# RWKV's block inverse on quarters of the array, transfers and norms set apart, and a new order of the jobs

## The chip, the cores and the metric

The kernel runs on one core of one Trainium2 chip. The metric is the device time of one execution in microseconds. TensorE is called PE here, VectorE DVE, ScalarE ACT, GpSimd POOL and SyncE SP; SP issues every DMA of this kernel.

## The reference, cut to what matters

Two layers of a decoder trunk over 512 tokens of width 1024. Five token mixers read columns of one input projection; their outputs are gated, merged, projected, normed and added to x.

```python
for l in range(DEPTH):                                   # DEPTH = 2
    h = rms_norm(x, norm_pre[l])
    cols = jnp.einsum('bsd,dn->bsn', h, w_in[l])         # 1024 x 9668
    ys = (rwkv7_branch(...), dsa_branch(...), retention_branch(...), s5_branch(...), memory_branch(...))
    merged = sum(gates[:, :, i] * jnp.einsum('bsw,wd->bsd', ys[i], w_branch[l, i]) for i in range(5))
    out = jnp.einsum('bsd,de->bse', merged, w_out[l])
    x = x + rms_norm(out, norm_post[l])

# rwkv7_branch, per token t and head:
sa = jnp.einsum('bhvk,bhk->bhv', state, -kk_t)
state = state * w_t + sa[..., None] * (kk_t * a_t) + v_t[..., None] * k_t
```

The RWKV state is carried in chunks of 128 tokens, which needs the inverse of a unit triangular 128 by 128 matrix for each of 4 heads and 4 chunks.

## The kernel before, in words

The program is written by a planner that runs while the kernel is built. `dense()` yields dense jobs (each one is a column block of a weight matrix times the 512 tokens), and `run()` puts steps of "lanes" between them: the branches, the setup, and the norms at a layer's end. The tables `ORDER` and `LANES` give the first order of jobs and lanes, `LAG` is how far ACT and DVE may lag behind PE before lanes pause. What comes out is one fixed order of instructions for each engine. A `yield` in a lane is a place where other work may come between.

A weight piece goes this way: SP loads 256 KB into one of 5 buffers `raw`; ACT casts it to `wh`, DVE subtracts to get the rest `wl` (4 buffers each); PE multiplies `wh` and `wl` with the high and low part of the tokens (`hh`, `hl`), three products that add up in PSUM. SP works in order: a DMA that has to wait for an engine or for a free buffer holds up all that stand behind it. So do DVE, ACT and POOL.

The places that the change touches:

- In `branch_rwkv` the inverse is built from 32 by 32 diagonal blocks (`X`, transposed into `Z`). The next level needs, for each of 4 matrices `u` and each half `b` of the 128 rows, the product of three 32 by 32 blocks. The kernel before multiplies whole 128 by 128 matrices (`N` with `Z`, then `X` with `W`), and masks the product with the constant `lev32`.
- `s5_tables` builds phase tables `sar` on POOL and DVE by doubling, stores them to DRAM (`s5tab`, four DMAs of 256 KB), and loads `sBt`. In the profile the small operands of the doubling are `sem`, `sea`, `seb` and `sta`.
- `finish_out` ends a layer for 128 tokens: `rs` (named `ors`) scales the projected row, `x` is updated, and `put_hT` norms it for the next layer: a square and sum on ACT (`xn`, `xrs`), a power on POOL, a scaled copy on DVE (`xn`), transposes on PE, and the split into `hh` and `hl`. Then `x` is stored to `xs`.
- At the very start, two tiles of x, the row `npre` and the constants are loaded, then five weight pieces.

Of the kernel before, what the change touches and what calls it, by code (L numbers as in the profile page):

```python
# [31 lines left out]
CW2 = float(np.float32(np.round((TWO_PI - CW1) * 2.0 ** 21) / 2.0 ** 21))  # L32
CW3 = float(np.float32(TWO_PI - CW1 - CW2))
MAGIC = 12582912.0
LAG = 11.5
EARLY = -1.0
MAXL = 6
NBUF = {"c1": 10, "c2": 14, "c4": 16, "c16": 2, "raw": 5, "w": 4}
ADD_G = 1.2
ORDER = ("rsg rv w wg g0 xq xsg di su dsg ssg dq g4 g2 dk mem1 dv g3 mem g1",  # L40
         "xsg dq g0 w di rsg wg g4 su dsg ssg dk dv g3 g1 g2")
LANES = ("ret idx>4 s5>4 ms1>3 rwkv dsa ms0 tab x>2", "idx>4 dsa>0 tab ret x rwkv>t s5")


def shape_constants():

    p = np.arange(128)
    c = {}
    c["ident"] = np.eye(128)
    up = (p[:, None] < p[None, :]) * 1.0  # L50
    c["upper"] = np.concatenate([up, up + np.eye(128)], 1)
    c["lev32"] = ((p[:, None] // 64 == p[None, :] // 64) & (p[:, None] % 64 < 32) & (p[None, :] % 64 >= 32)) * 1.0
    c["lower"] = (p[:, None] > p[None, :]) * 1.0
    c["causal"] = np.where(p[None, :] <= p[:, None], 0.0, NEG)
    inv = (10000.0 ** (-np.arange(32, dtype=np.float32) / np.float32(32))).astype(np.float32)
    c["invf"] = inv[p % 32][:, None]
    sgn = np.where(p % 64 < 32, -1.0, 1.0)
    c["sgn"] = sgn[:, None]
    sel = np.zeros((128, 2, 128))
    for j in range(2):  # L60
        for h in range(4):
            sel[h, j] = (p // 64 + 2 * j == h)
    c["sel"] = sel.reshape(128, 256)
    c["bo2"] = (p[:, None] // 64 == np.arange(2)[None, :]) * 1.0
    hd = RET_LOGG[2 * np.arange(2)[None, :] + p[:, None] // 64]
    c["qdec"] = np.exp(hd[:, :, None] * (p + 1)[None, None, :]).reshape(128, 256)
    c["kdec"] = 0.125 * np.exp(hd[:, :, None] * (127 - p)[None, None, :]).reshape(128, 256)
    rel = p[None, :] - p[:, None]
    c["rdecay"] = np.concatenate([np.where(rel >= 0, np.exp(RET_LOGG[2 * j + q] * np.maximum(rel, 0)), 0.0) * 0.125
                                  for q in range(2) for j in range(2)], 1)  # L70
    names = list(c)
    offs, o = {}, 0
    for n in names:
        offs[n] = (o, c[n].shape[1])
        o += c[n].shape[1]
    return np.concatenate([c[n] for n in names], 1).astype(np.float32), offs
# [146 lines left out]
def hybrid_kernel(ctx: ExitStack, tc: tile.TileContext, x, mem, positions, norm_pre, norm_post, norm_mem, w_in,  # L223
# [55 lines left out]
        return t  # L279

    x0 = [load_x(0, 0)]
    ncst = COFF["qdec"][0]
    cst = cp.tile([128, ncst], F32, name="cst")
    nci = COFF["ident"][1]
    assert COFF["ident"][0] == 0 and CONST.shape[1] == ncst + 1024
    SY.dma_start(cst[:, :nci], const[:, :nci])
    x0.append(load_x(0, 1))
    npre = {0: bcast_row(norm_pre[0], "npre")}

    def K(n):  # L290
        o, w = COFF[n]
        return cst[:, o:o + w]
# [810 lines left out]
            yield  # L1103


    def wsb(name, shape, dt=F32, bufs=2):
        return sb(name, shape, dt, bufs, "r")

    def rwkv_epi(l, t0):

# [17 lines left out]
    def branch_rwkv(l):  # L1128
# [87 lines left out]
        rks = sb("wrks", [128, 4, 4])  # L1216
        V.tensor_copy(rks, pss)
        yield
        lev = K("lev32")
        upper = K("upper").rearrange("p (a t) -> p a t", a=2)  # L1220
        M = [wsb("wM", [128, 2, 128]) for _ in range(2)]
        Ms = wsb("wMs", [128, 2, 128])
# [58 lines left out]
        for c in range(4):  # L1281
# [10 lines left out]
                T.transpose(ps[:, u, :], X[:, u, :], ident)  # L1292
            A.copy(Z, ps)
            yield
            ps = psb((128, 4, 128))
            for u in range(4):
                T.matmul(ps[:, u, :], N[u], Z[:, u, :])
            W = wsb("wW", [128, 4, 128])
            V.tensor_tensor(W, ps, lev[:, None, :].to_broadcast([128, 4, 128]), op=OP.mult)
            yield  # L1300
            ps = psb((128, 4, 128))
            for u in range(4):
                T.matmul(ps[:, u, :], X[:, u, :], W[:, u, :])
            V.tensor_tensor(Z, ps, Z, op=OP.add)
            ps = psb((128, 2, 2, 128))
            for a, src in enumerate((B, Kt)):
                for j in range(2):
# [122 lines left out]
    def s5_tables(l):  # L1430
# [35 lines left out]
        for r_ in range(2):  # L1466
            for b in range(2):
                SY.dma_start(s5d["tab"][2 * l + b][:, r_], tab[r_][:, 4 * b:4 * b + 4].rearrange("p b m -> p (b m)"))

        Bt = sb("sBt", [128, 2, nb, 16])  # L1470
        Cs = sb("sCs", [128, 2, nb, 16])
        for r_, w in enumerate((s5_b_re, s5_b_im)):
            bv = w[l].rearrange("(b q) p c -> q p b c", q=2)
            for q in range(2):
                SY.dma_start(Bt[64 * q:64 * q + 64, r_], bv[q])
        yield
        for b in range(2):
# [301 lines left out]
    def finish_out(l, i):  # L1779

        u, rr, xi = (a[i % 2] for a in ST[l, "fin", i // 2])
        rs = sb("ors", [128, 1])
        V.tensor_tensor(rs, rr[:, 0:1], rr[:, 1:2], op=OP.add)
        V.scalar_tensor_tensor(rs, rr[:, 2:3], 16e-6, rs, op0=OP.add, op1=OP.add)
        rsq(rs, rs)
        yield
        for a in range(2):
            o = slice(512 * a, 512 * a + 512)
            V.scalar_tensor_tensor(xi[:, o], u[:, o], rs, xi[:, o], op0=OP.mult, op1=OP.add)
            if l == L - 1:  # L1790
                yield
                SY.dma_start(outr[:, i, o], xi[:, o])
        if l < L - 1:
            yield from put_hT(l + 1, i, xi)
            SY.dma_start(xs[:, i, :], xi)

# [100 lines left out]
    def first_h(i):  # L1897
        if i >= 2:
            x0.append(load_x(0, i))
            yield  # L1900
        yield from put_hT(0, i, x0[i])

    lanes = [Lane(lambda i=i: first_h(i), ("t01",) if i > 1 else (), f"t0{i}", c4=2 + (i == 0)) for i in range(4)]
    lanes += [Lane(setup, ("t01",), "setup", c2=3, c4=4)]
# [89 lines left out]
```

## Time and profile before

| what | value |
|---|---|
| median of 3 runs | 1432.06 us (1430.72 to 1433.5) |
| profiled execution, its own time | 1431.76 us |
| span of the profiled execution | 1430.0 us |
| PE busy | 1373.7 us, 96% |
| DVE, ACT, POOL busy | 950.2 us, 558.3 us, 279.1 us |
| mean granted clock of PE | 0.986 |

How to read it: the span runs from the first to the last instruction, and the own time has some 1.8 us around it. Busy PE time counts also time in which PE ran at half its clock, where an instruction takes twice as long. In the rows, a product of fp32 operands shows as two MATMULs ("x8" for four products); the three-part products of `wh`, `wl` show as one each.

### The profile page before, as it was taken

The page shows a single profiled execution, that of the slowest core. Times are in us where ns is not written, and L with a number is a line of the kernel's source. Part 1 is how long each engine was busy: PE and PEld are TensorE (multiplying, and loading weights), DVE is VectorE, ACT ScalarE, POOL GpSimd, SP SyncE. Part 2 cuts the span into 40 slices and gives each one's busy share as a digit, 9 for nine tenths or more (in the row PEclk, how much of TensorE's full clock was granted, in tenths as well). Part 3 has the DMA queues.
Part 4 walks back from the last instruction along what each step waited for, and adds up shares of the span by engine and source line. Part 5 has one row for each costly group of instructions (what it writes and reads, how often), then busy time and mean ns, then how long its engine had stood idle before and what let it go on. Part 6 is the DMA issues. An engine that isn't in the chain of part 4 may idle for free.

```text
span 1430.0 us, 21718 instructions
## 1 busy us (share of the span) xinstructions
PE 1373.7 (96%) x7774; PEld 1147.8 (80%) x7774; DVE 950.2 (66%) x2027; ACT 558.3 (39%) x1196; POOL 279.1 (20%) x329
## 2 busy tenths in 40 slices
PE   5999999999999999999979899999999999999997
PEld 5878777788878887888979788687888788778887
DVE  5677565978867864444666567668788786844465
ACT  5433445333334235233554452443323332344353
POOL 0194241000111111110019523210010112411000
PEclk9999899999999999999999899999999999999999
DMA  6644425364242432344656624263534322422355
GB/s 193 176 114 127 122 89 141 89 184 126 72 121 74 129 101 52 89 118 125 188 152 177 180 78 134 60 143 94 141 103 147 89 67 72 114 67 81 99 163 181
DMA packets 243414, 170.60 MB, mean 119 GB/s; under 512 B 27657, under 2 KB 228331, under 8 KB 243307
## 3 DMA queue, kind: packets, MB, share of 16 engines
q1 hardware_dynamic: 243307, 169.22, 42.6%
q8 instruction: 61, 1.00, 0.3%
q14 instruction: 46, 0.38, 0.1%
HBM read 144.53 MB, written 18.87 MB: 114 GB/s over the span
## 4 chain that ended last, share of the span: by engine, by line
PE 82%; DVE 6%; POOL 4%; DMA 3%; ACT 2%; issue 2%; SPq 1%; POOLq 0%; DVEq 0%; ACTq 0%
PE d L209 62%; PE b L209 19%; DVE wl L209 2%; POOL sar L209 2%; DMA raw<-in_w_out_dram 1%; POOL sta L209 1%; DMA raw<-in_w_in_dram 1%; DVE x L209 1%; SPq L209 1%; ACT wh L209 0%; DMA posi<-in_positions_dram 0%; DMA x<-in_x_dram 0%; DMA rsw<-rq 0%; POOL sem L209 0%; POOL rsw L209 0%
## 5 line engine op out<-in xcount | busy, mean ns | idle before, releaser
L209 PE MATMUL d<-hh,wh 128*128 128x512 f32 (+2 forms) x1232 | 488.3, 396 | 13.5 <-ACT wh L209 13.5
L209 PE MATMUL d<-hh,wl 128*128 128x512 f32 (+2 forms) x1232 | 474.3, 385 | 6.6 <-DVE wl L209 6.5
L209 PE MATMUL d<-hl,wh 128*128 128x512 f32 (+2 forms) x1232 | 472.1, 383 | 0.0
L209 DVE TENSOR_TENSOR wl<-raw,wh 128x512 fp32r<-128x512 f32 x448 | 334.0, 761 | 139.2 <-ACT wh L209 135.6
L209 ACT CAST wh<-raw 128x512 fp32r<-128x512 f32 x448 | 268.7, 617 | 165.6 <-PE d L209 111.9
L209 PEld LDWEIGHTS d<-hh,wh 128*128 128x128 f32 (+1 forms) x1232 | 235.6, 191 | 73.1 <-issue 15.0
L209 PEld LDWEIGHTS d<-hh,wl 128*128 128x128 f32 (+1 forms) x1232 | 234.8, 191 | 58.4 <-DVE wl L209 10.1
L209 PEld LDWEIGHTS d<-hl,wh 128*128 128x128 f32 (+1 forms) x1232 | 235.8, 191 | 42.3 <-issue 0.5
L209 POOL TENSOR_TENSOR mg<-mg,gth 128x512 f32<-128x512 f32 x48 | 69.9, 1457 | 486.2 <-DVE gth L209 486.2
L209 DVE SCALAR_TENSOR_TENSOR gth<-gth,d 128x512 f32<-128x512 f32 x64 | 43.9, 686 | 107.2 <-PE d L209 103.4
L209 ACT ACTIVATE gth<-d 128x512 f32<-128x512 f32 (+1 forms) x90 | 51.9, 577 | 159.7 <-PE d L209 155.0
L209 PE MATMUL b<-wh,mgs 128*128 128x256 f32 x320 | 63.2, 283 | 5.6 <-ACT wh L209 4.1
L209 PE MATMUL d<-yl,wh 128*128 128x512 f32 x160 | 62.9, 393 | 0.7 <-DVE yl L209 0.7
L209 PE MATMUL d<-yh,wl 128*128 128x512 f32 x160 | 62.8, 393 | 0.0
L209 PE MATMUL d<-yh,wh 128*128 128x512 f32 x160 | 62.7, 392 | 0.0
L209 PEld LDWEIGHTS b<-wh,mgs 128*128 128x128 f32 x320 | 52.1, 190 | 6.3 <-ACT wh L209 4.3
L209 DVE MAX8 dm<-dac 128x8 f32<-128x256 f32 (+2 forms) x96 | 52.8, 550 | 0.1
L209 DVE MATCH_REPLACE8 dac<-dm,dac 128x256 f32<-128x256 f32 (+2 forms) x96 | 52.1, 543 | 0.0
L209 PE MATMUL b<-wl,mgs 128*128 128x256 f32 x160 | 45.5, 285 | 0.3 <-DVE wl L209 0.3
L209 POOL TENSOR_TENSOR ors<-ors,mhalf 128x1 f32<-128x1 f32 x8 | 5.0, 634 | 203.3 <-DVE ors L209 203.3
L209 PE MATMUL d<-wh,mgs 128*128 128x256 f32 x192 | 40.6, 285 | 2.0 <-DVE ou L209 2.0
L209 POOL TENSOR_TENSOR rsw<-rsw,sinT 128x1024 f32<-128x1024 f32 (+1 forms) x12 | 29.7, 2480 | 44.0 <-DMA rsw<-diq 20.7
(399 smaller groups left out, 2067.9 us busy)
## 6 DMA issues: line engine op xcount, KB each, us to landing
raw<-in_w_in_dram SPq DMA_DIRECT2D x324, 256.0 KB, 3.4
raw<-in_w_out_dram SPq DMA_DIRECT2D x64, 256.0 KB, 4.7
raw<-in_w_branch_dram SPq DMA_DIRECT2D x40, 256.0 KB, 3.2
x<-in_x_dram SPq DMA_DIRECT2D x8, 512.0 KB, 6.0
raw<-in_w_mem_kv_dram SPq DMA_DIRECT2D x16, 256.0 KB, 2.9
s5tab<-sar SPq DMA_DIRECT2D x8, 256.0 KB, 2.0
s5Wi<-sar SPq DMA_DIRECT2D x4, 512.0 KB
nn<-wNt SPq DMA_DIRECT2D x8, 256.0 KB
```

The source lines that it names most:

```text
L209: r = f(*args, **kw)
```

## The change

Three edits in the code, one in the constants, and new tables:

- The 32-level of the inverse multiplies just the 32 by 32 blocks that are not zero. `quarters` issues 8 products per stage: for each matrix `u` a pair (`b` = 0, 1) that lies on different rows and different columns of the array. The results are copied out 32 partitions at a time, one half by DVE, the other by ACT; the mask `lev32` and the addition to `Z` go.
- `yield`s are added: after each pair of `s5tab` stores, between the `sBt` loads, and in `finish_out` between the update of x and its norm.
- At the start, `npre` is loaded ahead of the constants and of the second x tile, and a first weight piece is prefetched (with its split) inside the first lane's norm.
- `LAG` goes from 11.5 to 10.5, and `ORDER` and `LANES` are new.

```diff
-LAG = 11.5
+LAG = 10.5
...
-ORDER = ("rsg rv w wg g0 xq xsg di su dsg ssg dq g4 g2 dk mem1 dv g3 mem g1",
...
+ORDER = ("xq rsg rv w g1 wg g3 xsg dsg di ssg su g4 dk dq dv mem1 mem g2 g0",
...
+LANES = ("ms1>3 tab ms0 s5 dsa>2 ret x rwkv idx>4", "ret s5>2 rwkv>4 x tab dsa>0 idx>2")
...
     x0 = [load_x(0, 0)]
+    npre = {0: bcast_row(norm_pre[0], "npre")}
     ncst = COFF["qdec"][0]
...
     x0.append(load_x(0, 1))
-    npre = {0: bcast_row(norm_pre[0], "npre")}
...
+    def quarters(mm):
+
+        sched.share = 0.5
+        for u in range(4):
+            for b in range(2):
+                T.matmul(*mm(u, b))
+        sched.share = 1.0
...
             A.copy(Z, ps)
             yield
-            ps = psb((128, 4, 128))
-            for u in range(4):
-                T.matmul(ps[:, u, :], N[u], Z[:, u, :])
-            W = wsb("wW", [128, 4, 128])
-            V.tensor_tensor(W, ps, lev[:, None, :].to_broadcast([128, 4, 128]), op=OP.mult)
-            yield
-            ps = psb((128, 4, 128))
-            for u in range(4):
-                T.matmul(ps[:, u, :], X[:, u, :], W[:, u, :])
-            V.tensor_tensor(Z, ps, Z, op=OP.add)
+
+            W = wsb("wW", [128, 4, 32], big=True)
+            q0, q1 = ([slice(64 * b + 32 * a, 64 * b + 32 * a + 32) for b in range(2)] for a in range(2))
+            pss = [psb((128, 4, 32)) for _ in range(2)]
+            quarters(lambda u, b: (pss[b][q0[b], u, :], N[u][q1[b], q0[b]], Z[q1[b], u, q1[b]]))
+            V.tensor_copy(W[q0[0]], pss[0][q0[0]])
+            A.copy(W[q0[1]], pss[1][q0[1]])
+            yield
+            pss = [psb((128, 4, 32)) for _ in range(2)]
+            quarters(lambda u, b: (pss[b][q0[b], u, :], X[q0[b], u, q0[b]], W[q0[b], u, :]))
+            V.tensor_copy(Z[q0[0], :, q1[0]], pss[0][q0[0]])
+            A.copy(Z[q0[1], :, q1[1]], pss[1][q0[1]])
...
         for r_ in range(2):
             for b in range(2):
                 SY.dma_start(s5d["tab"][2 * l + b][:, r_], tab[r_][:, 4 * b:4 * b + 4].rearrange("p b m -> p (b m)"))
+            yield
...
             for q in range(2):
+                yield
                 SY.dma_start(Bt[64 * q:64 * q + 64, r_], bv[q])
...
         if l < L - 1:
+            yield
             yield from put_hT(l + 1, i, xi)
...
-        yield from put_hT(0, i, x0[i])
+        for n, _ in enumerate(put_hT(0, i, x0[i])):
+            if n == 1 and i == 1:
+                prefetch(0, 0)
+            yield
```

How the new order stands on the engines at the passage from layer 0 to layer 1. First SP, where the tables of layer 1 (`s5tab`) are stored among the weight loads (`raw`). Before:

```order
L209 DMA xs<-x 128x1024 x2
L209 DMA raw<-in_w_in_dram 128x2x256 x3
L209 DMA raw<-in_w_in_dram 128x4x128 x11
L209 DMA s5tab<-sar 128x512 x4
L209 DMA sBt<-in_s_b_re_dram 64x8x16 x2
L209 DMA sBt<-in_s_b_im_dram 64x8x16 x2
L209 DMA raw<-in_w_in_dram 128x4x128
```

The same place of the change:

```order
L208 DMA raw<-in_w_in_dram 128x4x128 x9
L208 DMA s5tab<-sar 128x512 x2
L208 DMA raw<-in_w_in_dram 128x4x128 x2
L208 DMA s5tab<-sar 128x512 x2
L208 DMA raw<-in_w_in_dram 128x4x128
L208 DMA raw<-in_w_in_dram 128x2x256 x2
L208 DMA sBt<-in_s_b_re_dram 64x8x16
L208 DMA raw<-in_w_in_dram 128x2x256 x2
L208 DMA sBt<-in_s_b_re_dram 64x8x16
L208 DMA raw<-in_w_in_dram 128x4x128 x2
```

Where eight DMAs stood in a row, weight loads now stand between the pairs. Counted from the last load of `w_out`, 27 weight loads stand ahead of the first `s5tab` store in the kernel before, and 25 in the change.

Next POOL, at the same passage: the scales `ors` and `xrs` of the norms and the first doublings of the tables `sar`. Before:

```order
L209 TENSOR_TENSOR ors<-ors,mhalf 128x1 x2
L209 MEMSET sar 128x8 x2
L209 COPY sem<-un 128x16
L209 TENSOR_TENSOR xrs<-xrs,mhalf 128x1 x2
L209 TENSOR_TENSOR sar<-sar,sem 128x8
L209 TENSOR_TENSOR sta<-sar,sem 128x8
L209 TENSOR_TENSOR sar<-sar,sta 128x8
L209 TENSOR_TENSOR sea<-sem 128x16
L209 TENSOR_TENSOR seb<-sem 128x8 x2
```

The change:

```order
L208 TENSOR_TENSOR ors<-ors,mhalf 128x1 x2
L208 MEMSET sar 128x8 x2
L208 COPY sem<-un 128x16
L208 TENSOR_TENSOR sar<-sar,sem 128x8
L208 TENSOR_TENSOR sta<-sar,sem 128x8
L208 TENSOR_TENSOR sar<-sar,sta 128x8
L208 TENSOR_TENSOR sea<-sem 128x16
L208 TENSOR_TENSOR seb<-sem 128x8 x2
```

The first doubling (eight rows, with two copies back into `sem`) now stands ahead of the two `xrs`.

Last DVE, the second pair of token tiles at the same passage: the update of x (`x<-ou,ors,x`), its norm (`xrs`) and the splits of weight pieces (`wl`). Before:

```order
L209 TENSOR_TENSOR wl<-raw,wh 128x512 x2
L209 SCALAR_TENSOR_TENSOR x<-ou,ors,x 128x512 x2
L209 TENSOR_SCALAR xrs<-xrs 128x1
L209 SCALAR_TENSOR_TENSOR x<-ou,ors,x 128x512 x2
L209 TENSOR_SCALAR xrs<-xrs 128x1
L209 TENSOR_TENSOR wl<-raw,wh 128x512 x3
L209 SCALAR_TENSOR_TENSOR xn<-x,xrs,npre 128x512 x4
```

The change:

```order
L208 TENSOR_TENSOR wl<-raw,wh 128x512
L208 SCALAR_TENSOR_TENSOR x<-ou,ors,x 128x512 x4
L208 TENSOR_TENSOR wl<-raw,wh 128x512 x2
L208 TENSOR_SCALAR xrs<-xrs 128x1
L208 TENSOR_TENSOR wl<-raw,wh 128x512
L208 TENSOR_SCALAR xrs<-xrs 128x1
```

Splits of weight pieces now stand between the update and each `xrs`; the first pair of tiles (`x` four times, `wl` twice, `xrs`, `wl`, `xrs`) has the same form.

## Rows read from the trace of the kernel before

**Rows 1.** The page: its first line, and part 1, busy us.

```profile
span 1430.0 us, 21718 instructions
PE 1373.7 (96%) x7774; PEld 1147.8 (80%) x7774; DVE 950.2 (66%) x2027; ACT 558.3 (39%) x1196; POOL 279.1 (20%) x329
```

**Rows 2.** Waits of PE: engine, what for, us in total, times, longest.

```profile
PE d L209 <- ACT wh L209: 13.5, 4, 8.4
```

**Rows 3.** Windows: width; PE, PEld, DVE, ACT, POOL busy; PEclk, DMA, GB/s.

```profile
159.77:170.01 10.24, 10.24 (x37) 8.98 (x37) 4.50 (x7) 4.67 (x13) 4.94 (x2) 0.50 0.29 79
...
719.55:722.97 3.42, 3.10 (x14) 3.10 (x15) 3.42 (x7) 1.10 (x3) 0.00 (x0) 0.50 0.46 137
750.27:753.69 3.42, 3.23 (x15) 3.23 (x16) 3.40 (x7) 1.24 (x3) 3.34 (x6) 0.50 0.64 190
787.82:798.06 10.24, 6.09 (x27) 5.87 (x28) 4.12 (x5) 3.54 (x7) 5.34 (x9) 0.50 0.97 264
```

**Rows 4.** Timeline of PE in a chunk of RWKV: start us, us, instruction.

```profile
305.38 0.40 PE L209 MATMUL d<-hh,wl 128*128 128x512 f32 x1
305.62 1.06 PE L209 MATMUL b<-wZ,wN 128*128 128x128 f32 x8
306.43 0.48 PE L209 MATMUL d<-hh,wh 128*128 128x512 f32 x1
...
314.22 0.68 PE L209 MATMUL b<-wZ,wN 64*64 64x64 f32 x8
314.82 0.50 PE L209 MATMUL d<-hh,wh 128*128 128x512 f32 x1
...
322.11 0.39 PE L209 MATMUL d<-yh,wl 128*128 128x512 f32 x1
322.43 0.71 PE L209 MATMUL b<-wAR,wta 64*128 64x128 f32 x8
323.07 0.50 PE L209 MATMUL d<-hh,wh 128*128 128x512 f32 x1
```

**Rows 5.** Instructions on tile wW, DVE: durations min, median, max.

```profile
L209 DVE TENSOR_TENSOR wW<-b,cst x8: 684/692/693, 306.7 to 1173.6; 128x512 f32<-128x512 f32 x8
```

**Rows 6.** Timeline of SP at the tables of layer 1.

```profile
752.49 21.66 SPq L209 DMA_DIRECT2D raw<-in_w_in_dram  x14
779.86 5.05 SPq L209 DMA_DIRECT2D s5tab<-sar  x4
...
787.81 2.66 SPq L209 DMA_DIRECT2D raw<-in_w_in_dram  x5
```

**Rows 7.** Timeline of PE after its three long waits at the passage.

```profile
719.15 0.38 PE L209 MATMUL b<-wh,mgs 128*128 128x256 f32 x1 [4.15 <-ACT wh L209]
...
749.73 0.39 PE L209 MATMUL d<-hh,wh 128*128 128x256 f32 x1 [2.99 <-ACT wh L209]
...
791.97 0.58 PE L209 MATMUL d<-hh,wh 128*128 128x256 f32 x1 [8.35 <-ACT wh L209]
```

**Rows 8.** Timeline of POOL: the tables of layer 1.

```profile
746.75 0.98 POOL L209 TENSOR_TENSOR xrs<-xrs,mhalf 128x1 f32<-128x1 f32 x1 [4.50 <-DVE xrs L209]
...
749.95 0.52 POOL L209 TENSOR_TENSOR sar<-sar,sem 128x8 f32<-128x8 f32 x1
...
755.16 0.21 POOL L209 TENSOR_TENSOR sar<-sar,sem 128x16 f32<-128x16 f32 x1
...
782.81 1.28 POOL L209 TENSOR_TENSOR sar<-sar,sta 128x512 f32<-128x512 f32 x1
```

**Rows 9.** Timeline of DVE at the first pair of token tiles.

```profile
713.30 1.41 DVE L209 SCALAR_TENSOR_TENSOR x<-ou,ors,x 128x512 f32<-128x512 f32 x2
...
719.13 0.69 DVE L209 TENSOR_TENSOR wl<-raw,wh 128x512 fp32r<-128x512 f32 x1 [0.35 <-ACT wh L209]
```

**Rows 10.** Timeline of DVE at the start.

```profile
8.83 0.15 DVE L209 TENSOR_SCALAR xrs<-xrs 128x1 f32<-128x1 f32 x1 [2.97 <-ACT xn L209]
```

**Rows 11.** Windows: the busiest 120 us of DVE; columns as in rows 3.

```profile
300.00:420.00 120.00, 120.00 (x696) 97.52 (x695) 98.20 (x229) 39.10 (x79) 10.26 (x10) 1.00 0.42 123
```

More of the change, by code (lines that the diff above doesn't have):

```diff
@@ L39 @@
 ADD_G = 1.2
-ORDER = ("rsg rv w wg g0 xq xsg di su dsg ssg dq g4 g2 dk mem1 dv g3 mem g1",
-         "xsg dq g0 w di rsg wg g4 su dsg ssg dk dv g3 g1 g2")
-LANES = ("ret idx>4 s5>4 ms1>3 rwkv dsa ms0 tab x>2", "idx>4 dsa>0 tab ret x rwkv>t s5")
+ORDER = ("xq rsg rv w g1 wg g3 xsg dsg di ssg su g4 dk dq dv mem1 mem g2 g0",
+         "w xsg g1 dq di rsg dv g0 ssg su g3 g4 wg dk g2 dsg")
+LANES = ("ms1>3 tab ms0 s5 dsa>2 ret x rwkv idx>4", "ret s5>2 rwkv>4 x tab dsa>0 idx>2")
 def shape_constants():
@@ L51, in shape_constants @@
     c["upper"] = np.concatenate([up, up + np.eye(128)], 1)
-    c["lev32"] = ((p[:, None] // 64 == p[None, :] // 64) & (p[:, None] % 64 < 32) & (p[None, :] % 64 >= 32)) * 1.0
     c["lower"] = (p[:, None] > p[None, :]) * 1.0
@@ L1103, in branch_dsa, with wsb @@
             yield
-    def wsb(name, shape, dt=F32, bufs=2):
-        return sb(name, shape, dt, bufs, "r")
+    def wsb(name, shape, dt=F32, bufs=2, big=False):
+        return sb(name, shape, dt, bufs, "r", big)
+    def quarters(mm):
[4 more added lines that the diff above has]
+        sched.share = 1.0
     def rwkv_epi(l, t0):
@@ L1218, in branch_rwkv @@
         yield
-        lev = K("lev32")
         upper = K("upper").rearrange("p (a t) -> p a t", a=2)
```

## The prediction

> **What bounds the kernel now.** I read the page first. PE is busy 1373.7 of 1430.0 us [rows 1], so at most 56.3 us of the span are idle time of PE; whatever the change gives comes from there, from PE work that gets shorter, or from stretches in which PE runs at half its clock. The reader should see there that DVE (66%), ACT (39%) and POOL (20%) are no bounds as a whole. They matter where they are late for PE.
>
> The list of waits says for what PE stands: four waits of 13.5 us in all for `wh`, the longest 8.4 [rows 2]. The timeline of PE puts three long ones at the passage from layer 0 to layer 1: 4.15, 2.99 and 8.35 us [rows 7]. A table of windows then gives the granted clock: each of these three waits is followed at once by a stretch at 0.50, which is 1.2 GHz, with PE busy 3.10, 3.23 and 6.09 us in it. One stretch at 0.50 has no wait before or in it: 159.77 to 170.01, PE busy in all 10.24 us [rows 3]. Half of the busy time in such a stretch is lost against the full clock: 1.5, 1.6, 3.0 and 5.1 us.
>
> Last I read why `wh` is late, on SP, POOL and DVE [rows 6, 8, 9]. It is told with the parts it concerns.
>
> **A. Quarters on PE.** There are 16 stages (4 chunks, 2 products, 2 layers). A stage was 8 MATMULs on the full array, and is now 16 of 32 by 32, in pairs. From the start of the old group to the start of the next instruction: 306.43 - 305.62 = 0.81 us, or 0.10 per MATMUL. A 64 by 64 group of 8 takes 314.82 - 314.22 = 0.60, or 0.075 each: half the columns save a quarter. Eight on pairs of half arrays take 323.07 - 322.43 = 0.64 [rows 4]. The trace has no pair of quarters, so I bound it. If a pair runs as one, a stage is 8 steps of at most 0.075 (0.60), or, drawing the line from 128 and 64 columns on to 32, of 0.0625 (0.50). If nothing overlaps, it is 16 such steps: 1.0 to 1.2. The pairs of half arrays overlap in part, being 128 columns wide like the full ones and taking 0.64 against 0.81. I take 0.60: 16 x (0.60 - 0.81) = **-3 us**; bounds 16 x -0.31 = -5 and 16 x +0.39 = +6.
>
> Going over to another form may cost too. The product just before the paired group starts 322.43 - 322.11 = 0.32 us ahead of it, the one before the full group 305.62 - 305.38 = 0.24 [rows 4]: 0.08 for the entry, so -2 instead of -3, inside the bounds. The Trainium skill, page "TensorEngine Tiling (Array Packing)", Key Properties, says that a change of the tiling mode drains the array; it gives no figure. This trace agrees that going in costs something, and by its 0.08 the sum would be 1.3 us worse.
>
> DVE loses 16 masks of 0.69 [rows 5] and 16 additions; DVE and ACT get 16 copies each, of a quarter as many elements per partition. I cost this at nothing: PE is the bound beside it and DVE has 21.8 us free in its busiest 120 [rows 11]. If that cover were gone it would still be a gain for DVE, but each stage now needs two `b` tiles of PSUM where one did; that is a rival below.
>
> **B. Stores of the tables.** SP issues the last of 14 `raw` loads at 752.49 + 21.66 = 774.15, some 1.55 us apart. Then it stands at `s5tab`, whose first pair is issued at 779.86, when POOL has `sar`; the second pair needs the `sar` that POOL ends at 782.81 + 1.28 = 784.09. Four `sBt` loads follow, and the next `raw` is issued at 787.81 [rows 6, 8]. PE has run out at 791.97 - 8.35 = 783.62 and starts 4.16 us after that issue [rows 7].
>
> In the changed order POOL does the first doubling ahead of the two `xrs`, not behind. It took from 749.95 to 755.16, 5.2 us, and before the `xrs` at 746.75 POOL was idle 4.50 [rows 8], so it fits there nearly for nothing. The chain of the tables ends some 5.2 us earlier: first half at 774.6, second at 778.9. Between the pairs stand two `raw`, and the first pair comes two loads (3.1 us) earlier on SP, at 771.1. The same 27 loads are then issued by about 778, the second pair at 778.9, and the next `raw` at 779.8. With the same 4.16 us PE has its operand at 784.0, 0.4 us after it would run out. I leave it 1 us: 8.35 - 1 = 7.35 less, and without the long wait the 3.0 us of half clock go too: **-10 us**. If everything goes, it is -11.4. If POOL's chain is not earlier (the doubling then only changes places with a wait), the next `raw` comes at 785.0, PE at 789.2, the wait is 5.6 and the clock still falls: -2.8.
>
> What is late next: the `sBt` loads and the products of the tables, which stand in a lane and not in front of PE; and the weight loads behind, which SP now spreads over more time.
>
> **C. Norms apart.** DVE updates x from 713.30 on (1.41 us for two halves), waits for the sum of the norm, updates the other tile, and comes to `wl` at 719.13; PE stands until 719.15 [rows 7, 9]. Now the four updates stand together and two `wl` follow: 713.30 + 2 x 1.41 = 716.1 for the first `wl`, 3.0 us earlier. The 4.15 wait shrinks by 2.7 (ACT may be late with `wh` by the rest). At the second pair of tiles the same form stands; half of 2.99 is taken, 1.5. Together 4.2. What of the half clock behind them (1.5 + 1.6) goes I can't read, because the trace has no wait between 1 and 2.9 us there; I take somewhat over half: **-6 us**, bounds 0 (the wait stands at ACT instead) and 4.15 + 2.99 + 3.1 = -10. On DVE `xrs` is now queued behind a `wl`; who waits is POOL with its power, then `xn` and the transposes of layer 1, some us ahead of their use.
>
> **D. The clock at 160.** Ahead of and in the stretch at 0.50, PE did transposes and narrow products of the lanes (37 instructions in 10.24 us, [rows 3]) with few dense ones between. The new order puts most of those transposes and products elsewhere among dense jobs, but it makes another run of narrow products later in the preparation of RWKV. I take more than half of 5.1: **-3 us**; bounds -5.1 and, for a second such stretch, +5.1.
>
> **E. The start.** The second x tile lands one load later, about 1.3 us as far as SP's pitch of 1.55 goes [rows 6]; but the first `xn` on DVE only waits for `xrs` at 8.83 [rows 10], and the new order puts both `xrs` before it, with the first split of weights earlier. I take **+1 us** (-0.6 to +2.5).
>
> **F. Everything else of the new order.** Tables `ORDER`, `LANES` and `LAG` move nearly all lanes. Of the 56.3 us in which PE is idle, 15.5 are the three waits [rows 7] and some 9 lie before the first `xrs` is ready [rows 10]; the other 32 are in small pieces. Both orders have such pieces, and I see no reason for fewer: **+2 us** (-6, a fifth of them gone, to +10, one more wait like the longest with its slow stretch).
>
> **Sum:** -3 - 10 - 6 - 3 + 1 + 2 = -19, against the profiled execution's own 1431.76 (1.76 more than its span, 0.3 below the median): 1412.8, so **1413 us**. Its own range is 1404 to 1421.
>
> **The rivals.**
>
> R1, the waits move instead of going. SP serves one more `raw` only when a buffer is free, and the half-full pipe after the tables makes PE wait at the next load; in 787.82 to 798.06 the DMA engines were already at 0.97 [rows 3]. For it: that number. Against it: 137 and 190 GB/s in the windows behind the first two waits, against 264 in the third. B then gives -3 and C -1: 1431.8 - 3 - 3 - 1 - 3 + 1 + 2 = **1425**.
>
> R2, the quarters don't overlap. Then A is +6 and the sum is **1422**. For it: 64 columns cost 0.075 against 0.10, so narrow products cost more than their columns; against it: the paired group's 0.64. The Trainium skill, same page, Instruction Overhead, says that on trn2 each matmul has some 60 cycles of overhead, so one column lasts as long as 60; the trace agrees in direction (64 columns at three quarters of 128), and by that rule a quarter has no gain of its own: only the pairing can pay.
>
> R3, the order pays back elsewhere: D reverses (+5 instead of -3) and F costs 10: 1412.8 + 8 + 8 = 1429, **no measurable change**.
>
> R4, slower. Two `b` tiles a stage come from the ring that one came from, and each is freed by a copy on DVE or ACT that queues behind splits of 0.69 or so [rows 5]. If PE stands at every one of the 16 stages for two such operations, 1.4 us, that is 22 us and the kernel takes **1435**; it decides from 1.2 us a stage on (19 / 16). For it: DVE is busy 98.2 of 120 us there [rows 11]. Against it: dense products of `d`, which lie in other tiles, stand between the stages [rows 4].
>
> **How the numbers follow.** The likeliest gets 0.60, R1 0.16, R2 0.10, R3 0.07, R4 0.07. The time is the likeliest's. The range, 1402 to 1427, leaves out R3 and R4 and a little below, in which the bounds of B and C meet. A change of 0.2% (2.9 us) is about what a measurement of this kernel can tell from none. Faster by more: 0.60 + 0.16 + 0.10 = 0.86; R3 is mostly within it, 0.06; slower 0.08.
>
> **What would show it.** In the profile after: the wait of PE at the tables at most 1 us instead of 8.35 and no 0.50 behind it (B); `sar` 128x8 on POOL ahead of `xrs`, and the second half of the tables done some 5 us sooner against the weight loads (B); the two waits at the norms below 2 us (C); the granted clock at 1.00 from 150 to 210 (D); a group of 32 by 32 products of about 0.6 us to the next start (A); first weight product within 2.5 us of its old time (E). Wrong it would be if PE's idle time stayed near 56 us in sum while these waits went, or if PE busy grew: then the order, not the places named, decides.

## The result, and the profile after

The change takes 1407.22 us (median of 4 runs, 1405.51 to 1411.81), the kernel before 1431.39 us beside it; the ratio is 0.9841, with a 95% interval of 0.9806 to 0.9876. That is 24 us faster, where 19 were predicted; 1407 lies in the range of 1402 to 1427 and in the likeliest case's own range.

The profiled execution of the change is the slowest of its four, 1411.81 us, and the one with the lowest granted clock (0.990, the others 0.992 to 0.995), so the terms are compared between the two profiled executions: 1431.76 to 1411.81, -20.0. The first line of the page of the change, and PE in part 1:

```profile
span 1410.0 us, 22005 instructions
...
PE 1362.2 (97%) x7902; PEld 1132.9 (80%) x7902; DVE 934.6 (66%) x2022; ACT 561.7 (40%) x1212; POOL 286.2 (20%) x334
```

Against [rows 1] PE's idle time goes from 56.3 to 1410.0 - 1362.2 = 47.8 us, and its busy time falls by 11.5. Which part of that is the clock, the windows at half clock tell. Of the change (columns as in rows 3), then of the kernel before the two such stretches that [rows 3] doesn't show, and the sum of the same view over all six between the start and the end:

```profile
26.94:33.77 6.83, 6.47 (x30) 6.35 (x31) 2.69 (x11) 2.09 (x5) 0.00 (x0) 0.50 0.98 257
177.13:180.54 3.41, 3.41 (x12) 2.28 (x9) 3.31 (x6) 0.44 (x2) 2.83 (x1) 0.50 0.35 87
719.85:723.26 3.41, 3.41 (x19) 3.41 (x17) 0.00 (x0) 0.00 (x0) 0.00 (x0) 0.50 0.89 272
805.18:812.00 6.82, 6.82 (x25) 5.30 (x24) 6.71 (x8) 1.02 (x4) 6.62 (x6) 0.50 0.36 91
832.48:835.90 3.42, 3.42 (x11) 2.83 (x11) 0.72 (x3) 3.29 (x12) 0.00 (x0) 0.50 0.01 2
sum 23.89, PE 23.53 PEld 20.17 DVE 13.43 ACT 6.84 POOL 9.45; mean PE 4.71 PEld 4.03 DVE 2.69 ACT 1.37 POOL 1.89
```

```profile
36.89:43.71 6.82, 5.48 (x26) 5.19 (x26) 5.50 (x12) 3.20 (x6) 0.00 (x0) 0.50 0.56 147
...
200.73:204.14 3.41, 3.41 (x10) 2.62 (x9) 1.36 (x4) 3.07 (x11) 3.21 (x6) 0.50 0.00 0
...
sum 37.55, PE 31.55 PEld 28.99 DVE 22.30 ACT 16.83 POOL 16.84; mean PE 5.26 PEld 4.83 DVE 3.72 ACT 2.80 POOL 2.81
```

Half of 31.55 - 23.53 is 4.0 us of clock. The other 7.5 us of PE's busy time are work that is no longer there. So -20 is 8.5 of idle time, 4.0 of clock and 7.5 of work.

The idle time didn't fall everywhere. The stretch from 100 to 250 us, a part of layer 0, before and then in the change:

```profile
100.00:250.00 150.00, 145.94 (x815) 118.02 (x814) 98.35 (x217) 69.94 (x166) 54.31 (x46) 0.95 0.41 116
```

```profile
100.00:250.00 150.00, 140.73 (x825) 113.62 (x824) 98.41 (x217) 68.99 (x166) 57.22 (x52) 0.99 0.42 113
```

PE is idle there for 150 - 140.73 = 9.3 us instead of 4.1, in waits of 1.0 to 1.7 us for `wl` (at 104, 155 and 168 us), `wh` (153) and a load of `xkm` (176).

The work is the quarters. Timeline of PE in the change, a chunk of RWKV (as rows 4):

```profile
309.14 0.39 PE L208 MATMUL d<-hh,wl 128*128 128x512 f32 x1
309.46 0.44 PE L208 MATMUL b<-wZ,wN 32*32 32x32 f32 x16
309.83 0.50 PE L208 MATMUL d<-hh,wh 128*128 128x512 f32 x1
```

From start to start a stage takes 0.37 us, where a group of whole products took 0.81 [rows 4], and 0.89 in the second stage of an inverse (309.29 to 310.18 in the kernel before).

The passage from layer 0 to layer 1: PE's long waits (as rows 7), SP at the tables (as rows 6) and POOL (as rows 8) of the change:

```profile
718.34 0.38 PE L208 MATMUL d<-wh,mgs 128*128 128x256 f32 x1 [1.89 <-DVE ou L208]
...
734.17 0.39 PE L208 MATMUL d<-hh,wl 128*128 128x256 f32 x1 [1.57 <-DVE wl L208]
...
768.69 0.39 PE L208 MATMUL d<-hh,wh 128*128 128x256 f32 x1 [2.83 <-ACT wh L208]
```

```profile
742.75 13.90 SPq L208 DMA_DIRECT2D raw<-in_w_in_dram  x10
763.45 0.81 SPq L208 DMA_DIRECT2D s5tab<-sar  x2
764.36 1.03 SPq L208 DMA_DIRECT2D raw<-in_w_in_dram  x2
767.25 0.81 SPq L208 DMA_DIRECT2D s5tab<-sar  x2
```

```profile
729.79 0.22 POOL L208 TENSOR_TENSOR sar<-sar,sem 128x8 f32<-128x8 f32 x1
...
735.57 1.49 POOL L208 TENSOR_TENSOR xrs<-xrs,mhalf 128x1 f32<-128x1 f32 x2
...
761.81 1.62 POOL L208 TENSOR_TENSOR sar<-sar,sta 128x512 f32<-128x512 f32 x1
...
765.96 1.26 POOL L208 TENSOR_TENSOR sar<-sar,sta 128x512 f32<-128x512 f32 x1
```

The 4.15 and 2.99 us for `wh` at the norms are gone; a 1.89 (DVE late with the scaled row `ou`) and a 1.57 stand near. The 8.35 at the tables is 2.83. SP still stands at the first pair of stores, from 756.65 to 763.45, longer than before; what is new is that two loads go out from 764.36 on, ahead of the second pair, for which it stands another 1.9 us (765.39 to 767.25).

### The profile page after: what moved, and what is told of

Same layout as the page of the kernel before. It is cut to its first block, busy times and chain, and to the rows that moved or that the text cites. A ratio compares the mean times of both kernels' runs of the same rounds, so it can differ in the third digit from the quotient of the medians.

```text
span 1410.0 us, 22005 instructions
## 1 busy us (share of the span) xinstructions
PE 1362.2 (97%) x7902; PEld 1132.9 (80%) x7902; DVE 934.6 (66%) x2022; ACT 561.7 (40%) x1212; POOL 286.2 (20%) x334
## 4 chain that ended last, share of the span: by engine, by line
PE 85%; DVE 5%; ACT 3%; POOL 3%; DMA 2%; issue 2%; SPq 0%; DVEq 0%; POOLq 0%; ACTq 0%
PE d L208 65%; PE b L208 19%; DMA raw<-in_w_out_dram 1%; DVE wl L208 1%; POOL sar L208 1%; ACT wh L208 1%; POOL sta L208 1%; DMA raw<-in_w_in_dram 1%; DVE wL L208 1%; DVE xmx L208 0%; DMA x<-in_x_dram 0%; DVE x L208 0%; SPq L208 0%; ACT sTp L208 0%; POOL seb L208 0%
```

## The experiments

An edit of a lane would make the planner lay out everything anew, so two effects would be mixed. In the runs marked "frozen", the sequence of job steps and lane steps that the planner chose is written into the kernel as a list and followed; `joined()` in place of a `yield` lets a step run on into the next, and the next turn of that lane is left out:

```diff
+            t = STEPS.pop(0)
+            if t in "JWE":          # a dense job's step, a wait of it, its end
+                ... next(dn) ...
+            if drop.get(t[1:], 0):
+                drop[t[1:]] -= 1
+                continue
+            pick = next(q for q in active if q.name == t[1:])
```

**Control.** The change, frozen, with nothing edited: the same instructions in the same order.

> The change with its order frozen and nothing else edited: the same instructions in the same order as the change. It is the base for the frozen runs with one edit undone, whose smaller differences (3 us) depend on it. Expected 1405 to 1410 us; if it came out at 1404 or below, the version with the tables started early (1408) would be slower than the change, and the old start and the moved doubling would cost more than 3 us each; at 1409 or above these three could not be told from the change.

Measured: 1409.36 us (1406.58 to 1413.04), ratio 0.9861 (0.9840 to 0.9883). The frozen runs are set against this ratio; 0.001 is 1.4 us. Each ratio's interval reaches some 0.002 to either side, so that of a difference of two reaches some 0.003, and one below 4 us is not told. As the expectation has it for that case, the smaller ones below stay open.

**Whole products in the new order.** The inverse from the kernel before, frozen in the change.

```diff
-            W = wsb("wW", [128, 4, 32], big=True)
-            ... quarters ...
+            ps = psb((128, 4, 128))
+            for u in range(4):
+                T.matmul(ps[:, u, :], N[u], Z[:, u, :])
+            ... mask with lev32, second product, addition to Z ...
```

> The change with its order of jobs and lane steps frozen, and only the 32-level of the inverse back on whole 128 by 128 products (with its mask). Theory P (quarters are a saving of PE's own): the groups take 0.81 to 0.89 us again instead of 0.37, so PE's work grows by 16 x 0.48 = 7.7 us and the time goes from 1407.2 to about 1415; idle time of PE stays as in the change, about 40 us between its first and last product. Rival S (the order makes the gain; PE work in the inverse lies beside waits of the lane): less than 3 us slower, with idle time of PE falling by what its work grows.

Measured: 1416.15 us, ratio 0.9903 (0.9878 to 0.9928), 6.0 us over the control. PE's idle time is 1411.9 - 1364.5 = 47.4, as in the change. The sum over this run's stretches at half clock gives its work:

```profile
sum 17.08, PE 15.23 PEld 13.34 DVE 8.92 ACT 6.82 POOL 3.97; mean PE 3.81 PEld 3.33 DVE 2.23 ACT 1.70 POOL 0.99
```

Without half of that, PE works 1364.5 - 7.6 = 1356.9 us, against 1362.2 - 11.8 = 1350.4 in the change: 6.5 us more. Theory P holds.

**Quarters in the old order.** The kernel before, frozen, with the inverse of the change.

```diff
-            ps = psb((128, 4, 128))
-            ... whole products ...
+            quarters(lambda u, b: (pss[b][q0[b], u, :], N[u][q1[b], q0[b]], Z[q1[b], u, q1[b]]))
+            ... copies, second stage ...
```

> The kernel before with its own order frozen, and only the inverse on quarters. Theory P: 7.7 us faster, about 1424, waits at the passage (4.2, 3.0, 8.4 us) unchanged. Rival S: less than 3 us, about 1430. If the two edits need each other (the quarters pay only in the new order), this run shows nothing while the full products in the new order cost 7.7.

Measured: 1422.56 us, ratio 0.9942 (0.9920 to 0.9964), 8.3 us faster. The waits at the passage stand (one view, waits of PE, of this run):

```profile
PE d L208 <- ACT wh L208: 13.4, 4, 8.2
...
PE b L208 <- ACT wh L208: 3.8, 1, 3.8
```

The quarters need no new order.

**Pairs taken apart.** The change, frozen.

```diff
-        for u in range(4):
-            for b in range(2):
+        for b in range(2):
+            for u in range(4):
                 T.matmul(*mm(u, b))
```

> The change, frozen, with the eight quarter products of a stage issued first all for b = 0, then all for b = 1, so that neighbours lie on the same rows and columns of the array. Theory P2 (neighbours on different rows and columns run at once, and that makes 0.37): a group takes 0.7 us or more, 16 x 0.35 = 5 to 6 us slower, 1412 to 1413. Rival N (a 32-column product is that short by itself, and the pair adds nothing): a group stays within 0.05 us of 0.37 and the time within 2 us of 1407.

Measured: 1413.16 us, ratio 0.9876 (0.9852 to 0.9900), 2.1 us over the control by the ratios, inside the noise. The timeline of PE tells it more finely:

```profile
311.58 0.59 PE L208 MATMUL b<-wZ,wN 32*32 32x32 f32 x16
312.10 0.50 PE L208 MATMUL d<-hh,wh 128*128 128x512 f32 x1
```

A group takes 0.52 us, so pairing gives 0.15 x 16 = 2.4 us. Neither expectation had it: pairs overlap, but two thirds of the saving of a stage (0.81 to 0.52) come from the narrow product itself. Neighbours on one tile of the array start 0.032 us apart in this run, where it was 0.112 for the 128 by 128 products and 0.058 for the 64 by 64 ones of the kernel before: nearly in proportion to the columns.

**Only the new tables.** The kernel before with the new `ORDER`, `LANES` and `LAG`, laid out anew by its planner.

```diff
-LAG = 11.5
+LAG = 10.5
-ORDER, LANES of the kernel before
+ORDER, LANES of the change
```

> The kernel before with nothing but the new ORDER, LANES and LAG; its planner makes the order for the old code. Rival S: nearly all of the gain, 1410 to 1414. Theory P with spacing: the new tables give the clock at 160 us (about -5) and little more, the waits at norms (4 and 3 us) and the long one at the tables (over 5 us) stand as before: 1422 to 1428.

Measured: 1432.11 us, ratio 1.0015 (0.9996 to 1.0034): nothing. The waits for `wh` are still there:

```profile
PE d L209 <- ACT wh L209: 11.7, 3, 7.3
```

Rival S falls, and so does the gain at 160 us that the other theory gave it: a stretch of 13.65 us at 0.50 stands at 210.58 in this order instead:

```profile
210.58:224.23 13.65, 12.90 (x44) 8.79 (x44) 12.19 (x21) 3.62 (x11) 4.11 (x5) 0.50 0.00 0
```

**Stores and loads of the tables in a row.** The change, frozen.

```diff
-            yield                       # after each pair of s5tab stores
+            joined()
...
-                yield                   # ahead of each sBt load
+                joined()
                 SY.dma_start(Bt[64 * q:64 * q + 64, r_], bv[q])
```

> The change, frozen, with the four s5tab stores and the four sBt loads of a layer issued in one row, where the change has the first pair. Theory B (spacing the stores is what shortened the wait of 8.35 us at the tables): SP stands through both pairs again; by the change's profile the second pair was issued at 767.25 and the loads behind it come after about 3.5 us more, so the next raw goes out near 771 instead of 764.4 and PE waits about 6 us longer, with a stretch at half clock behind it: 6 to 9 us slower, 1413 to 1416. Rival O (the chain on POOL, not the spacing, sets it): less than 2 us slower.

Measured: 1414.66 us, ratio 0.9898 (0.9877 to 0.9918), 5.3 us over the control. SP, and PE behind it, and the window with the half clock:

```profile
764.33 4.59 SPq L208 DMA_DIRECT2D s5tab<-sar  x4
...
771.82 2.73 SPq L208 DMA_DIRECT2D raw<-in_w_in_dram  x5
```

```profile
775.77 0.58 PE L208 MATMUL d<-hh,wh 128*128 128x256 f32 x1 [9.03 <-ACT wh L208]
```

```profile
771.51:781.75 10.24, 5.98 (x26) 5.75 (x27) 3.37 (x5) 3.54 (x7) 0.00 (x0) 0.50 0.83 215
```

The stores go out about when they did (764.33 against 763.45), and the next `raw` at 771.82 instead of 764.36. PE starts 3.95 us after it. The wait is the old one again, with its slow stretch. Theory B holds as far as the spacing goes; the 5.3 us lie a little under its 6 to 9, by less than can be told.

**The first doubling behind `xrs`.** The change, frozen, two steps of the tables' lane moved behind the two `xrs`.

```diff
-POOL: ... sar x3, sea, seb x2, sem x2 (first doubling), xrs x2, sar 128x16 ...
+POOL: ... xrs x2, sar x3, sea, seb x2, sem x2 (first doubling), sar 128x16 ...
```

> The change, frozen, with the first doubling of layer 1's tables moved on POOL from ahead of the two xrs to behind them, as in the kernel before. Theory B as predicted (the chain on POOL ends 5.2 us earlier for it): the stores come about 5 us later, PE's wait at the tables grows from 2.8 to about 8 us: 5 to 8 us slower. Rival O2 (the doubling changes places with a wait): the chain ends within 1 us of where it did, the time within 1.5 us of 1407.

Measured: 1410.33 us, ratio 0.9869 (0.9846 to 0.9893), 1.1 us over the control, not told from it. In the trace:

```profile
733.24 1.44 POOL L208 TENSOR_TENSOR xrs<-xrs,mhalf 128x1 f32<-128x1 f32 x2 [5.12 <-DVE xrs L208]
```

```profile
741.71 13.79 SPq L208 DMA_DIRECT2D raw<-in_w_in_dram  x10
764.10 0.81 SPq L208 DMA_DIRECT2D s5tab<-sar  x2
```

```profile
769.24 0.58 PE L208 MATMUL d<-hh,wh 128*128 128x256 f32 x1 [4.59 <-ACT wh L208]
```

```profile
734.66 0.21 POOL L208 TENSOR_TENSOR sar<-sar,sem 128x8 f32<-128x8 f32 x1
...
736.22 0.22 POOL L208 TENSOR_TENSOR sar<-sar,sem 128x16 f32<-128x16 f32 x1
```

POOL now idles 5.12 us ahead of `xrs`, yet counted from the row of ten weight loads the first pair of stores is only 764.10 - 741.71 - (763.45 - 742.75) = 1.7 us later, and PE's wait 1.8 us longer. The 5.2 us of the prediction are mostly not in the order of POOL: behind `xrs` the first doubling takes 736.22 - 734.66 = 1.6 us, where it takes 735.57 - 729.79 = 5.8 ahead of it in the change. Rival O2 is nearer, if not within its 1 us. This run has a slow stretch at the wait, from 768.10 on, with PE busy 5.69 us, which the change hasn't; its time doesn't show it.

**Update and norm in one step.** The change, frozen.

```diff
         if l < L - 1:
-            yield
+            joined()
             yield from put_hT(l + 1, i, xi)
```

> The change, frozen, with the update of x and its norm again in one step, so that DVE waits at xrs between the two tiles before it comes to the splits of weights. Theory C: PE waits about 4 us and 3 us again at the two pairs of tiles, now 0 to 2: 4 to 7 us slower, 1411 to 1414. Rival M (the splits run ahead far enough in this order): less than 2 us slower.

Measured: 1417.69 us, ratio 0.9918 (0.9899 to 0.9936), 8.2 us over the control. PE's waits at the passage in this run, and windows:

```profile
710.31 0.38 PE L208 MATMUL b<-wh,mgs 128*128 128x256 f32 x1 [2.29 <-ACT wh L208]
...
742.67 0.58 PE L208 MATMUL d<-hh,wh 128*128 128x256 f32 x1 [4.25 <-ACT wh L208]
```

```profile
711.36:714.78 3.42, 3.42 (x18) 3.42 (x17) 2.75 (x5) 0.46 (x1) 0.00 (x0) 0.50 0.59 196
725.02:728.43 3.41, 3.41 (x19) 3.41 (x18) 0.87 (x2) 0.00 (x0) 0.00 (x0) 0.50 0.73 207
742.08:748.91 6.83, 6.24 (x28) 6.02 (x29) 3.29 (x8) 2.79 (x8) 6.02 (x22) 0.50 0.57 151
```

Both waits are back, the first shorter than the 4 us expected, each with a slow stretch; the one in the middle stands behind the wait of 1.89 us for `ou`, as in the change. So theory C holds; 8.2 us is a little over its 4 to 7. The wait at the tables is gone in this run: PE, being late, no longer overtakes the stores.

**The old start.** The change, frozen.

```diff
-    npre = {0: bcast_row(norm_pre[0], "npre")}      # ahead of cst
...
     x0.append(load_x(0, 1))
+    npre = {0: bcast_row(norm_pre[0], "npre")}
...
-            if n == 1 and i == 1:
-                prefetch(0, 0)
```

> The change, frozen, with the old start: constants and the second x tile ahead of npre, no piece prefetched inside the first norm. My prediction took the new start as a loss of 1 us; the trace of the change shows PE's first weight product at 14.3 us against 15.3. Theory E2 (the new start gains): about 1 us slower, 1408. Rival E1: 1 us faster. Both are near what can be told; the start of the first weight product in the trace decides.

Measured: 1410.23 us, ratio 0.9859 (0.9834 to 0.9884): no difference from the control. The first weight product starts here, and below it in the change:

```profile
15.91 0.58 PE L208 MATMUL d<-hh,wh 128*128 128x256 f32 x1 [1.19 <-ACT wh L208]
```

```profile
14.32 0.56 PE L208 MATMUL d<-hh,wh 128*128 128x256 f32 x1
```

The new start is 1.6 us earlier there. That much can't be seen in the time.

**All edits undone in the new order.** Whole products, stores in a row, update and norm in one step, old start, frozen in the change's order.

```diff
-            quarters(...)                  # both stages
+            T.matmul(ps[:, u, :], N[u], Z[:, u, :])    # whole products, mask, addition
-            yield                          # s5tab, sBt, finish_out
+            joined()
-                prefetch(0, 0)             # and npre behind the second x tile
```

> The change's order of jobs and lane steps frozen, with all four code edits undone (full products, stores in one row, update and norm in one step, old start). If the parts add: 1407.2 + 8.9 + 7.4 + 10.5 + 3.0 = 1437, slower than the kernel before. If the waits at the norms hide the wait at the tables (with the norm edit alone undone the trace shows no wait at the tables): 1430, as before and as the new tables alone with a fresh plan (1432).

Measured: 1429.19 us, ratio 0.9999 (0.9984 to 1.0013): the time of the kernel before. Against the control the four edits together are worth 0.0138, 19.7 us, and one by one 6.0 + 5.3 + 8.2 + 0 = 19.5. My expectation's 1437 had added differences of medians against 1407.2; by the ratios, each with its own runs of the kernel before beside it, and against the control, the parts add up. That they do so within 0.2 us is chance, since each is known to some 4 us. The windows at half clock in this run, those of layer 0 and then the sum over all seven:

```profile
155.90:159.31 3.41, 3.41 (x19) 3.41 (x18) 2.20 (x14) 0.89 (x2) 0.76 (x1) 0.50 0.01 2
176.38:183.21 6.83, 5.77 (x17) 4.27 (x18) 6.32 (x11) 2.90 (x5) 5.04 (x2) 0.50 0.49 136
...
sum 37.56, PE 30.60 PEld 27.77 DVE 18.94 ACT 14.78 POOL 9.40; mean PE 4.37 PEld 3.97 DVE 2.71 ACT 2.11 POOL 1.34
```

**All edits by hand in the old order.** The kernel before, frozen, with the quarters, one weight load between the pairs of stores, the norm two job steps behind the update, and the new start.

```diff
+            quarters(...)                  # both stages, with their copies
+            yield 2                        # between the pairs of s5tab: 2 job steps later
+                yield 1                    # between the sBt loads
+            yield 2                        # between update and norm
+                prefetch(0, 0)             # and npre ahead of cst
```

> The kernel before with its old order of jobs and lanes frozen, and all edits of the code put in by hand: quarters, the stores of the tables in two pairs with a weight load between, the norm some weight splits behind the update of x, and the new start. Only ORDER, LANES and LAG, and where each lane step stands, are still the old ones. Theory L (local edits make the gain, the new tables next to nothing): the quarters alone gave 8.6 and the parts undone one by one in the change cost 7.4 (stores), 10.5 (norms) and 3.0 (start), so even if those overlap, 1403 to 1412. Rival W (the spacing pays only with the places that the new order gives): 1417 to 1422, little better than the quarters alone; at the tables PE then waits 5 us or more, because POOL's chain is as late as before.

Measured: 1417.84 us, ratio 0.9915 (0.9895 to 0.9936), 12.2 us faster; the 3.9 more than the quarters alone gave are just under what can be told. That is rival W's range. Its mechanism is there in part: PE waits 2.95 and then 1.91 us at the tables (776.58 and 780.96). But the old order also keeps its slow stretch at 160 us:

```profile
157.06:167.30 10.24, 10.24 (x38) 9.08 (x38) 4.57 (x8) 4.50 (x13) 4.94 (x2) 0.50 0.32 84
```

**Tables started early.** The change, frozen, with the twenty doubling steps of layer 1's tables taken up to 26 job steps forward, and their lane opened when the first half of layer 0's projection is done.

```diff
-        "tab": Lane(lambda l=l: s5_tables(l), ("trig",) if l == 0 else ("out01",), ...
+        "tab": Lane(lambda l=l: s5_tables(l), ("trig",) if l == 0 else ("out00",), ...
```

> The change, frozen, with the twenty steps that double the tables of layer 1 started while layer 0's projection still runs (after its first two token tiles), where POOL is idle for 19.5 us; the stores keep their place on SP. Theory B: the tables are done before SP comes to the stores, SP no longer stands, and PE's wait of 2.8 us and what clock loss follows it go: 2 to 5 us faster, 1402 to 1405. Rival Q (SP's loads are limited by free buffers, not by the stores): no difference; or slower, if POOL's work slows DVE's part of the norms.

Measured: 1408.15 us, ratio 0.9851 (0.9830 to 0.9872), not told from the change or the control. POOL has the second half ready at 751.89 + 1.63 = 753.52, SP doesn't stand any more, and PE has no wait at the tables:

```profile
751.89 1.63 POOL L208 TENSOR_TENSOR sar<-sar,sta 128x512 f32<-128x512 f32 x1
```

```profile
745.22 13.49 SPq L208 DMA_DIRECT2D raw<-in_w_in_dram  x10
758.75 0.97 SPq L208 DMA_DIRECT2D s5tab<-sar  x2
```

So at the tables the mechanism is as theory B says, but over the runs the 2 to 5 us expected don't show. The profiled execution is short (span 1402.9 against 1410.0 and 1411.3), but mostly for the clock: it is the fastest of its four runs, while those of the change and the control are their slowest, and the sum over its stretches at half clock is small:

```profile
sum 10.24, PE 10.24 PEld 10.24 DVE 3.87 ACT 1.30 POOL 1.56; mean PE 3.41 PEld 3.41 DVE 1.29 ACT 0.43 POOL 0.52
```

Against the change, (23.53 - 10.24) / 2 = 6.6 of the 7.1 us are clock. PE's idle time, 1402.9 - 1356.0 = 46.9, is only 0.9 below the change's 47.8, and 4.0 below the control's 1411.3 - 1360.4 = 50.9, though those two run the same instructions. So what the wait of 2.83 us is worth over the runs stays open.

## Why the prediction was right, point by point

The direction, the time and the range were right. That the sum of -19 comes so near the -20 between the two profiled executions is partly luck: A, D and E gave 8.6 us more than their terms, B and F 7.5 less. By its own steps, between these two executions:

- **A, quarters: -3 predicted, -7.5 measured** in PE's work (6.0 in time when undone). The term was mis-sized, beyond its lower bound of -5. The step that failed is the price of a narrow MATMUL, taken from the length of the 64 by 64 group (0.60 for 8) and drawn on to 0.0625 for 32 columns. The pitch within that group is only 0.058, so 0.60 - 8 x 0.058 = 0.14 of its length is for going in and out and doesn't grow with the count; at 32 columns the pitch is 0.032. So 16 MATMULs of 32 columns, not in pairs, take 0.52, less than those 8, and in pairs 0.37. Also the old groups of the second stages took 0.89, not the 0.81 that all 16 were priced at. R2 is out. The Trainium skill, page "TensorEngine Tiling (Array Packing)", Instruction Overhead, gives each matmul some 60 cycles on trn2, so that one column lasts as long as 60. What the prediction drew from it, that a quarter has no gain of its own, fails here: two thirds of a stage's saving come without pairing. The rule itself these runs don't test, since 60 cycles at 2.4 GHz are 0.025 us (an estimate from the page's figure), and a pitch of 0.032 us is above that. The product just ahead of the group starts 309.46 - 309.14 = 0.32 before it, as in [rows 4], so the entry costs the 0.08 us that the prediction named.
- **B, tables: -10 predicted, -8.5 measured** (8.35 - 2.83 = 5.5, and the 3.0 of clock). Spacing was the right mechanism (5.3 us when it is undone). One step failed: how much earlier POOL's chain ends. SP came to the stores 9.2 us before PE ran dry (756.65 and 765.86), much as I had it (771.1, and some 780.5 for the 26th load, two loads of 1.55 before 783.62). But it stood there 6.8 us and not 3.5, so the 26th load went out at 764.36, only 1.5 us before PE ran dry. The doubling ahead of `xrs` brings the stores 1.7 us, not 5.2: its 5.2 us were its length at one place, and in the run that puts it back it takes 1.6. That is close to the prediction's own fallback, in which the doubling only changes places with a wait; it had a wait of 5.6 us there, and 2.83 came. Nor is the 3.0 of clock sure to go: behind the same wait of 2.83 us the run with the old start has a slow stretch of 3.41 us (at 774.44).
- **C, norms: -6 predicted.** In the profile 4.15 + 2.99 become 1.57, and the 1.89 takes the place of a 0.73; with one slow stretch (1.7 us) instead of two (3.2) that is 5.57 - 1.16 + 1.5 = 5.9 less. Undoing it cost 8.2. Here term and mechanism held.
- **D, the clock at 160: -3 predicted, -5.1 measured** between these two executions: 10.24 and 3.41 us at half clock (159.77 and 200.73) became 3.41 (177.13), (13.65 - 3.41) / 2. The sign named for it, a clock of 1.00 from 150 to 210, didn't come. The gain belongs to the new order, since the profiled runs of the old one (the kernel before, the quarters alone, all edits by hand) keep the long stretch near 158. But it isn't the same size in each execution: the frozen runs of the new order have between 3.4 and 13.7 us of such stretches from 100 to 200 us, so the term is anything from nothing to -5, and -3 is as good a value as the runs allow. And the prediction left out what this costs: from 100 to 250 us PE's idle time grows by 5.2 us, as much as the clock gives. That does stand in each execution: 8.8 to 11.5 us of idle time there in the nine frozen runs of the new order, 4.1 and 4.3 in the two of the old.
- **E, the start: +1 predicted, -1.0 measured** in the trace (first weight product at 15.32 before and 14.32 after; 15.91 with the old start in the new order). Sign wrong, size below what the time can tell. I priced the later x tile, and gave too little for the earlier split, which takes away PE's wait of 1.19 for the first `wh`.
- **F, the rest: +2 predicted, about +8** as what is left: -20 + 7.5 + 8.5 + 5.9 + 5.1 + 1. The waits from 100 to 250 us are 5.2 of it, two new slow stretches at 805 and 832 are (6.82 + 3.42) / 2 = 5.1, and a new wait of 1.70 us for `wl` stands just ahead of the first (until 803.28); against that, idle time fell by 3.6 from 20 to 100 us and by 1.7 from 250 to 690. The two slow stretches are mostly a matter of this execution: of the nine frozen runs in the new order only the control has both, and six have neither. Against the medians, -24, the rest would be about +4.

Rival R1 came true in part, 2.83 us of the wait staying, though not for want of buffers: with the tables early it goes. Some waits did move: the places named in B, C and E lost 5.5 + 4.4 + 1.0 us of idle time, the whole kernel 8.5. R4's waits for a second `b` tile don't appear: the list of waits of the change has none for a stage of the inverse. Three readings in the prediction are off without moving its sum: DVE loses 8 masks and 8 additions, not 16 of each ([rows 5] has x8); the third slow stretch begins within its wait (787.82, the wait lasts until 791.97); and DVE's busiest 120 us lie rather at 250 to 370, with 100.4 us.

What the prediction did not see is how order and edits hang together. The new order alone gives nothing, frozen (0.9999) or laid out anew (1.0015). With all edits undone its profile shows where it goes: in layer 0 PE is busy 3.41 + 5.77 = 9.2 us at half clock instead of 5.48 + 13.65 = 19.1, which saves 5.0; from the passage on it is 30.60 - 9.18 = 21.4 instead of 12.4 [rows 3], which costs 4.5; and its idle time is 1429.9 - 1372.4 = 57.5 instead of 56.3. On top of that order the edits give 19.7 us, on top of the old one 12.2. What makes the norms and stores yield less in the old order is only partly shown (the waits of 2.95 and 1.91).

## What to carry to other kernels

When a transfer waits for a slow chain in the same queue as the weight loads, first put loads between the waiting transfers; the wait can cost twice, once as idle time and again as a slow stretch (waits of 8.35 and 9.03 us had one here, one of 2.83 in the change had none). Price a smaller product by the pitch within its group, not by the group's length, which holds the cost of going in and out. Take an instruction's cost at the place where it will stand, not its length where it stands now. Freeze the order before undoing an edit: a planner that lays out everything anew mixes the edit with its own choices, and an order that is worth nothing alone may be what lets the edits pay.

## What was not expected of the hardware

Sixteen fp32 MATMULs of 32 by 32 take 0.52 us in a row and 0.37 in pairs on different rows and columns of the array, against 0.60 for eight of 64 by 64. The same instructions in the same order fall to half clock in other places from one execution to the next: at 177.13 in the profiled execution of the change, at 155.03 in that of the control. The same two `seb` instructions of 128 by 8 take 2.56 us on POOL in the change (at 732.22) and 0.36 in the run with the doubling behind `xrs` (at 735.45); why is not shown.
